# Sample-state updates of a hybrid decoder step: from the shared K/V projection into the third feed-forward

## The chip, the cores and the metric

The kernel runs on one core of a Trainium2 chip. The metric is the device time of one execution in microseconds; the time before is the median of three runs. A TensorE matmul engine (PE), VectorE (DVE), ScalarE (ACT), GpSimd (POOL) and SyncE (SP) run side by side, each with an instruction queue of its own that it takes in order. SP only issues DMAs here; POOL computes and issues DMAs.

## The reference

One inference step of a two-layer decoder over 512 prompt tokens and 8 sample sequences of 4 tokens each, with model width 1024. Each layer is feed-forward, mixer, feed-forward. The mixer of layer 0 is a gated linear attention (GLA) with a recurrent state, that of layer 1 an attention over shared keys and values, which are projected once from the residual stream after layer 0. What matters here is the new GLA state of the samples, an output of the step:

```python
b = jnp.cumsum(gi, axis=2)
b_last = b[:, :, -1:, :]
...
S = jnp.exp(b_last)[:, :, 0, :, None] * S + jnp.einsum('bhcd,bhce->bhde', ki * jnp.exp(b_last - b), vi)
```

For each of 8 sequences and 4 heads a state of 128 x 256 (f32) is scaled by row and a product of keys and values over the 4 tokens is added. The states come from `state_gla` and go to output 6, 4.2 MB each way. Nothing later in the step reads them. The feed-forwards compute `(silu(a) * b) @ w_down` with `a, b = split(u @ w_up)`, and hidden width 2816 = 22 x 128.

## The kernel before, in words

All activations stand with features on the partitions and the 544 tokens (512 + 32) along the free axis, in two halves of 272. Full-precision products are made of three fp32r matmuls, from a high and a low part of each operand: `halves` (L156 to L158) rounds on ACT and subtracts on DVE.

The order of the work is feed-forward "00", GLA, feed-forward "02", shared K/V projection, feed-forward "10", attention, feed-forward "12".

**State work.** `state_stacks` (L1374 to L1386) splits the keys `kts` and the values `vs` of the samples, which GLA left behind, into high and low parts and stacks them on 96 partitions, with 12 casts on DVE (L1384, `kstk`) and 12 on ACT (L1385, `vstk`). `state_step` (L1395) has 16 calls, each with two sequences of one head. At the first call of a head POOL makes the keys masked by sequence, for all 8 sequences at once (L1400, `km`, 96 x 1024, one buffer). For each of two sequences then PE multiplies masked keys with values (L1408, into the PSUM bank `pus`, two banks) and DVE scales the old state and adds (L1409). Every second call stores four states (L1411) and loads the next four but one (L1393), both from POOL's queue; the state tiles hold four sequences, in two buffers.

**Where it stands.** `proj_tokens` (L911) works through five column chunks of the K/V weights with five token blocks each, and runs one of the 16 state steps ahead of each block from the second on (`extra`). What follows a block are the head norms (`norm_heads`, L1437 on: squares on ACT, sums, reciprocal square roots and scaling on DVE, a factor on POOL, and transposes on PE four blocks later) and the stores of keys and values. The weights are loaded by SP and split by `halves` (`hkv`, `lkv`).

**The feed-forward.** `ffn_seven` (L513) treats three of the 22 hidden blocks plainly (the head: `plain_up`, both halves, 6 x 48 matmuls) and the others by a seven-product scheme in place of eight products (`seven`, L679). In the head it also makes sums and differences of the input quarters (`inputs`, L551, and `last_input`, L570). `late` keeps the third of these in short-lived tiles and computes it again in `last_input`, instead of holding it in `t3`. In the main part a hidden block has seven products of 12 matmuls, into five PSUM banks, and after each product `between` (L795) runs some of the down blocks of the round before (each followed by a DVE update of the residual, L398) and a `tick`. `slots` is the number of buffers for the gated values; the sixteen down blocks are spread over the first `7 * (slots - 3)` calls of `between`, 21 at most.

**Steps in a feed-forward.** `steps` are pieces of other work which `tick` (L520) runs: one at each of the first four ticks, and then so many that they are spread evenly over all 139 ticks. The first six ticks are in the head, one after each half of a plain block. Feed-forwards "00" and "02" carry the conditioning projections in this way, with `slots=5, late=True`; "10" has no steps, six slots and is not late.

The instructions are put on each engine's queue by a scheduler that goes by readiness and by program order, so neighbouring parts interleave. A tile of a pool starts when the tile that had its place is done.

Of the kernel before, what the change touches and what calls it, by code (L numbers as in the profile page):

```python
# [9 lines left out]
F32 = mybir.dt.float32  # L10
F32R = mybir.dt.float32r
# [4 lines left out]
ALU = mybir.AluOpType  # L16
AX = mybir.AxisListType

P = 128
# [18 lines left out]
C_SEQ = 640  # L38
# [56 lines left out]
def mod(l, sub, which):  # L95
    return 88 * l + 24 * sub + 8 * which
# [3 lines left out]
def trunk_kernel(ctx: ExitStack, tc: tile.TileContext, a, out, dbg=None, stop=None):  # L100
    nc = tc.nc
    V, S, G, PE, SP = nc.vector, nc.scalar, nc.gpsimd, nc.tensor, nc.sync
# [10 lines left out]
    def aux_bank(name):  # L113
        return pp.tile([P, 512], F32, tag="aux", name=name, bufs=2)
# [21 lines left out]
    cst = keep.tile([P, C_N], F32, name="cst")  # L136
# [50 lines left out]
    ebl = gs_pool.tile([P, 4, 12], F32, name="ebl")  # L187
# [104 lines left out]
    start = ExitStack()  # L292
# [66 lines left out]
    def stats(name, half):  # L359
        t0, t1 = HALF[half]  # L360
        ps = aux_bank(f"st{name}")
        for i, o in enumerate((0, 128, 144)):
            for j in range(3):
                PE.matmul(ps[:, i:i + 1], lhsT=accs[half][j][:, o:o + 128], rhs=ones[:, 0:1], start=j == 0, stop=j == 2)
        x = mean_eps(f"nx{name}", ps[:, 0:3], 3)
        y = rsqrt(x[:], 3, "nr")
        spread(name, y, [(0, P, 0, t0, 128), (1, P, 0, t0 + 128, 128), (2, P, 112, t0 + 256, 16)])
# [39 lines left out]
    def after(name, shift, scale):  # L407
        def f(half):
            stats(f"{name}{half}", half)
            if half:  # L410
                make_u(name, half, shift, scale)
                return []
            return [lambda k=k: make_u(name, half, shift, scale, k, k + 1) for k in range(NB)]
        return f
# [584 lines left out]
    slots = [ada_tile] * 4 + [lo32, hi32] * 2 + [raw_tile] * 2 + [lo32, hi32] * 2 + [ada_tile] * 2  # L999
# [22 lines left out]
    late = [ada_half_loads(v, 1, slots) for v in range(2)]  # L1022
# [349 lines left out]
    stk = {}  # L1372

    def state_stacks(gs_pool2):  # L1374
        kh, kl = (tmp.tile([P, HA], F32R, tag="nv", name=f"kts{i}", bufs=3)[:, 0:P] for i in range(2))
        vh, vl = (tmp.tile([P, HA], F32R, tag="sq", name=f"vs{i}", bufs=3)[:, 0:256] for i in range(2))
        halves(kh, kl, kts[:])
        halves(vh, vl, vs[:])
        ks = gs_pool2.tile([96, 4, P], F32R, name="kstk")
        vt = gs_pool2.tile([96, 4, 256], F32R, name="vstk")  # L1380
        for i, (x, y) in enumerate(((kh, vh), (kh, vl), (kl, vh))):
            for hd in range(4):
                r, o = slice(32 * hd, 32 * hd + 32), slice(32 * i, 32 * i + 32)
                V.tensor_copy(out=ks[o, hd], in_=x[r, :].bitcast(F32))  # L1384
                S.copy(vt[o, hd], y[r, :].bitcast(F32))  # L1385
        stk["k"], stk["v"] = ks, vt  # L1386

    def state_load(gs_pool2, i):
        if i < 8:
            hd, bh = divmod(i, 2)  # L1390
            t = gs_pool2.tile([P, 1024], F32, tag="s1", name=f"s1_{hd}_{bh}", bufs=2)
            stk["s", i] = t[:].rearrange("p (b e) -> p b e", b=4)
            G.dma_start(out=stk["s", i], in_=a["state_gla"][0, 4 * bh:4 * bh + 4, hd].rearrange("b d e -> d b e"))  # L1393

    def state_step(gs_pool2, hd, bh, pr):  # L1395
        if bh == 0 and pr == 0:
            if hd == 0:
                state_stacks(gs_pool2)
            km = gs_pool2.tile([96, 8, P], F32R, tag="km", name=f"km{hd}", bufs=1)
            G.tensor_tensor(out=km[:], in0=stk["k"][:, hd].bitcast(F32).unsqueeze(1).to_broadcast([96, 8, P]),  # L1400
                            in1=cst[0:96, C_SEQ:C_SEQ + 8].unsqueeze(2).to_broadcast([96, 8, P]), op=ALU.mult)
            stk["m"] = km
        st = stk["s", 2 * hd + bh]
        pu = aux_bank(f"pus{hd}_{bh}_{pr}")
        for i in range(2):
            b = 4 * bh + 2 * pr + i
            o = pu[:, i * 256:i * 256 + 256]
            PE.matmul(o, lhsT=stk["m"][:, b], rhs=stk["v"][:, hd], start=True, stop=True)  # L1408
            V.scalar_tensor_tensor(out=st[:, 2 * pr + i], in0=st[:, 2 * pr + i], scalar=ebl[:, hd, 4 + b:5 + b], in1=o, op0=ALU.mult, op1=ALU.add)  # L1409
        if pr:  # L1410
            G.dma_start(out=out[6][0, 4 * bh:4 * bh + 4, hd].rearrange("b d e -> d b e"), in_=st)  # L1411
            state_load(gs_pool2, 2 * hd + bh + 2)

    seq1 = ada_seq(range(11, 20))
    ffn_seven("02", 0, 1, mod(0, 2, 2), after("kv", 72, 80), seq1[:-2], held=seq1[-2:], slots=5, late=True)
# [44 lines left out]
    with ExitStack() as es:  # L1460
        kp = es.enter_context(tc.tile_pool(name="kvt", bufs=1))
        gk = kp.tile([P, 64], F32, name="gk")
        bfv = kp.tile([P, 16], F32, name="bfv")
        SP.dma_start(out=gk[:], in_=a["g_k"].partition_broadcast(P))
        SP.dma_start(out=bfv[:], in_=a["b_f"].partition_broadcast(P))
        ks_out = out[7].rearrange("b t h d -> (b t) (h d)")
        vs_out = out[8].rearrange("b t h d -> (b t) (h d)")
        k_out = out[3][0].rearrange("t h d -> t (h d)")
        v_out = out[4][0].rearrange("t h d -> t (h d)")
        V.memset(lf[:], 0.0)  # L1470

        def evac_kv(ci, t, ps):
            if ci < 2:
                def emit(x, xT):
                    SP.dma_start(out=k_out[t * P:(t + 1) * P, ci * 512:(ci + 1) * 512], in_=x)
                    kx = [kp.tile([P, 512], F32R, tag=f"kx{i}", name=f"kx{ci}_{t}_{i}", bufs=3) for i in range(2)]
                    halves(kx[0][:], kx[1][:], xT)
                    hv, lv = (v[:].bitcast(F32).rearrange("p (k t) -> p k t", k=4) for v in kx)
                    SP.dma_start(out=khscr[:].rearrange("(k p) t -> p k t", p=P)[:, 4 * ci:4 * ci + 4, t * P:(t + 1) * P], in_=hv)
                    for e in range(2):  # L1480
                        SP.dma_start(out=klscr[e::2, 0:64].rearrange("k p t -> p k t")[:, 4 * ci:4 * ci + 4, t * P:(t + 1) * P], in_=lv[64 * e:64 * e + 64])
                return norm_heads(kp, f"k{ci}_{t}", ps, 8, gk, emit)
            c0, w = VC[ci - 2]
            x = kp.tile([P, 352], F32, tag="vx", name=f"vx{ci}_{t}", bufs=2)
            S.copy(x[:, 0:w], ps[:, 0:w])
            SP.dma_start(out=v_out[t * P:(t + 1) * P, c0:c0 + w], in_=x[:, 0:w])
            SP.dma_start(out=vscr[t * P:(t + 1) * P, c0:c0 + w], in_=x[:, 0:w])
            if ci == 4:
                V.tensor_tensor(out=lf[:, t], in0=ps[:, w:w + 16], in1=bfv[:], op=ALU.add)

        def evac_kvs(ci, ps):
            if ci < 2:
                def emit(x, xT):
                    for j in range(4):
                        SP.dma_start(out=ks_out[:, ci * 512 + j * P:ci * 512 + (j + 1) * P], in_=x[32 * j:32 * j + 32])
                    V.tensor_copy(out=kTs[:, 4 * ci:4 * ci + 4], in_=xT.rearrange("p (j t) -> p j t", j=4))
                return norm_heads(kp, f"ks{ci}", ps, 2, gk, emit)
            quads(vnew, ps, *VC[ci - 2])
            if ci == 4:
                V.tensor_tensor(out=lf[0:32, 4], in0=ps[0:32, 256:272], in1=bfv[0:32], op=ALU.add)  # L1500

        gs_pool2 = es.enter_context(tc.tile_pool(name="gsv2", bufs=1))
        for i in range(2):
            state_load(gs_pool2, i)
        st_steps = [lambda hd=hd, bh=bh, pr=pr: state_step(gs_pool2, hd, bh, pr) for hd in range(4) for bh in range(2) for pr in range(2)]
        nv = {(hf, k): kp.tile([P, HA], F32, name=f"nv10_{hf}_{k}") for hf in range(1) for k in range(NB)}
        left = proj_tokens("kv", a["w_kvf"], [[(0, 512)], [(512, 512)], [(1024, 352)], [(1376, 352)], [(1728, 320), (2048, 16)]], evac_kv, evac_kvs, (4, 0, 1, 2, 3), st_steps)
        assert not left
        for (hf, k), v in nv.items():
            scaled(v, hf, mod(1, 0, 1), k)  # L1510
        for hf in range(2):
            make_u("10", hf, mod(1, 0, 0), mod(1, 0, 1), ready=None if hf else nv)
        for j in range(4):
            G.dma_start(out=vs_out[:, 256 * j:256 * j + 256], in_=vnew[32 * j:32 * j + 32, :])
# [62 lines left out]
    if stop == "kv":  # L1577
        return

    ffn_seven("10", 1, 0, mod(1, 0, 2), after("11", mod(1, 1, 0), mod(1, 1, 1)))  # L1580
    dump("h3", h[:])


# [313 lines left out]
```

## Time and profile before

| | |
|---|---|
| median of three runs | 2404.79 us (2399.41 to 2405.72) |
| profiled execution: device time | 2402.91 us |
| its span from first to last instruction | 2401.1 us, mean granted PE clock 0.98 |
| busy: PE, weight loads, DVE, ACT, POOL | 2298.5, 2141.6, 1828.6, 982.0, 923.0 us |
| first and last state matmul (L1408) | start at 1208.5 and 1284.1 us |
| matmuls of the K/V projection | from 1173.1 to 1313.0 us |
| matmuls of feed-forward "10" | from 1313.4 to 1691.5 us |
| DMA bytes in the whole span | 319.45 MB |

A row of a group reads: line, engine, operation, output tile <- input tiles, shape, count | busy us in all, mean ns of one | us in which the engine stood idle just before, and who released it. A row of waits reads: who waited <- for whom: us in all, how many times, the longest. Matmuls are pipelined, so the time from one start to the next is what a matmul costs, and not its duration.

### The profile page before, as it was taken

Reading aid. Unit: us, or ns where it says so; the run is one execution under the profiler, and the core shown is the slowest. Engines: PE = TensorE matmul, PEld = TensorE weight load, DVE = VectorE, ACT = ScalarE, POOL = GpSimd, SP = SyncE. Lnnn points to the kernel's source line nnn. Section 1 sums busy time; section 2 is a strip of 40 time slices with the busy share of each in tenths; the row PEclk is TensorE's granted clock in tenths of the full one; section 3 lists DMA queues with packets and bytes.
Section 4 is the critical chain, followed back from the end, with each engine's and each line's share of the span. In section 5 each row is a group of like instructions: output and inputs, shape, how many; then the busy total and the mean of one; then the engine's idle time right before and its main releaser. Section 6 shows DMA issues by size and latency. Waiting matters only on the chain. (4 is left out here: it accounts for less than half of the span.)

```text
span 2401.1 us, 49301 instructions
## 1 busy us (share of the span) xinstructions
PE 2298.5 (96%) x19292; PEld 2141.6 (89%) x19292; DVE 1828.6 (76%) x3881; ACT 982.0 (41%) x1831; POOL 923.0 (38%) x960
## 2 busy tenths in 40 slices
PE   7999999998999999999989999999999799999999
PEld 6899999987979999999769999999796479999999
DVE  6887777749556987777795988888757667888887
ACT  3343333444533443333524444434436544444432
POOL 0355544207102365444241355543324212455452
PEclk8999999999999999999999999999899899999999
DMA  8535555322172445555467233332146751233322
GB/s 306 172 124 193 192 187 178 114 69 62 54 219 64 141 129 181 187 174 174 144 203 246 81 104 94 99 94 88 47 111 185 157 164 52 78 104 89 102 84 78
DMA packets 356894, 319.45 MB, mean 133 GB/s; under 512 B 25247, under 2 KB 317949, under 8 KB 356614
## 3 DMA queue, kind: packets, MB, share of 16 engines
q1 hardware_dynamic: 341734, 300.24, 40.0%
q0 software_dynamic: 14928, 16.06, 3.0%
q8 instruction: 152, 2.49, 0.4%
q14 instruction: 80, 0.66, 0.1%
HBM read 298.17 MB, written 18.38 MB: 132 GB/s over the span
## 5 line engine op out<-in xcount | busy, mean ns | idle before, releaser
L178 PE MATMUL pd<-gh,ld 128*128 128x272 f32 x1408 | 408.6, 290 | 3.3 <-DVE ld L158 3.3
L176 PE MATMUL pd<-gh,hd 128*128 128x272 f32 x1408 | 409.2, 291 | 2.5 <-ACT hd L157 2.5
L177 PE MATMUL pd<-gl,hd 128*128 128x272 f32 x1408 | 409.3, 291 | 2.2 <-POOL gl L677 2.2
L176 PE MATMUL p<-uh,hu 128*128 128x272 f32 x1216 | 351.8, 289 | 0.0
L177 PE MATMUL p<-ul,hu 128*128 128x272 f32 x1216 | 350.9, 289 | 0.0
L178 PE MATMUL p<-uh,lu 128*128 128x272 f32 x1216 | 350.8, 288 | 0.0
L158 DVE TENSOR_TENSOR lu<-rua,hu 128x512 fp32r<-128x512 f32 (+1 forms) x228 | 272.2, 1194 | 45.9 <-ACT hu L157 37.7
L157 ACT CAST hu<-rua 128x512 fp32r<-128x512 f32 (+1 forms) x228 | 174.0, 763 | 290.4 <-PE p L177 131.8
L398 DVE SCALAR_TENSOR_TENSOR h<-pd,mods,h 128x240 f32<-128x240 f32 (+1 forms) x512 | 240.5, 476 | 49.7 <-PE pd L178 48.9
L178 PEld LDWEIGHTS pd<-gh,ld 128*128 128x128 f32 x1408 | 268.3, 191 | 3.9 <-DVE ld L158 3.9
L176 PEld LDWEIGHTS pd<-gh,hd 128*128 128x128 f32 x1408 | 268.4, 191 | 3.5 <-ACT hd L157 2.7
L177 PEld LDWEIGHTS pd<-gl,hd 128*128 128x128 f32 x1408 | 268.5, 191 | 3.0 <-POOL gl L677 3.0
L176 PE MATMUL p<-th,hu 128*128 128x272 f32 x912 | 264.5, 290 | 1.8 <-ACT th L157 1.8
L178 PE MATMUL p<-th,lu 128*128 128x272 f32 x912 | 264.2, 290 | 0.0
L177 PE MATMUL p<-tl,hu 128*128 128x272 f32 x912 | 264.0, 290 | 0.2 <-DVE tl L158 0.2
L403 POOL TENSOR_TENSOR h<-h,gs 128x32 f32<-128x32 f32 x256 | 127.9, 499 | 333.9 <-DVE gs L401 333.6
L176 PEld LDWEIGHTS p<-uh,hu 128*128 128x128 f32 x1216 | 229.3, 189 | 6.2 <-issue 2.1
L177 PEld LDWEIGHTS p<-ul,hu 128*128 128x128 f32 x1216 | 229.4, 189 | 0.0
L178 PEld LDWEIGHTS p<-uh,lu 128*128 128x128 f32 x1216 | 228.9, 188 | 0.0
L639 POOL TENSOR_TENSOR s<-rua,rub 128x512 f32<-128x512 f32 x76 | 115.1, 1514 | 244.6 <-DMA rub<-in_w_ffn_up_dram 131.3
L645 POOL TENSOR_TENSOR rua<-rub,rua 128x512 f32<-128x512 f32 x76 | 101.2, 1332 | 225.0 <-DVE lu L158 130.2
L176 PEld LDWEIGHTS p<-th,hu 128*128 128x128 f32 x912 | 172.4, 189 | 6.1 <-ACT th L157 2.0
(543 smaller groups left out, 6007.4 us busy)
## 6 DMA issues: line engine op xcount, KB each, us to landing
adaw<-in_w_ada_dram SPq DMA_DIRECT2D x128, 512.0 KB, 4.5
rua<-in_w_ffn_up_dram SPq DMA_DIRECT2D x88, 512.0 KB, 3.9
rub<-in_w_ffn_up_dram SPq DMA_DIRECT2D x88, 512.0 KB, 3.8
rd<-in_w_ffn_down_dram SPq DMA_DIRECT2D x96, 384.0 KB, 3.3
adah<-in_w_ada_dram SPq DMA_DIRECT2D x16, 512.0 KB, 6.3
adaw<-in_w_ada_kv_dram SPq DMA_DIRECT2D x16, 512.0 KB, 8.2
rd<-in_w_ffn_down_dram SPq DMA_DIRECT2D x32, 256.0 KB, 2.7
kp<-in_cache_k_dram SPq DMA_DIRECT2D x16, 512.0 KB, 11.9
```

The source lines that it names most:

```text
L157: S.copy(hi, src)
L158: V.tensor_tensor(out=lo, in0=src, in1=hi.bitcast(F32), op=ALU.subtract)
L176: PE.matmul(ps, lhsT=wh, rhs=xh, start=first and i == 0, stop=False)
L177: PE.matmul(ps, lhsT=wh, rhs=xl, start=False, stop=False)
L178: PE.matmul(ps, lhsT=wl, rhs=xh, start=False, stop=last and i == n - 1)
L398: V.scalar_tensor_tensor(out=h[:, m, t0:p1], in0=ps[:, 0:n], scalar=mods[:, gate + m, 0:1], in1=h[:, m, t0:p1], op0=ALU.mult, op1=ALU.add)
L403: G.tensor_tensor(out=h[:, m, TP:T], in0=h[:, m, TP:T], in1=st[:], op=ALU.add)
L639: G.tensor_tensor(out=o["s3"][:], in0=a11, in1=a21, op=ALU.subtract)
L645: G.tensor_tensor(out=a11, in0=a21, in1=a11, op=ALU.subtract)
```

## The change

The state work leaves the K/V projection and becomes 17 steps of feed-forward "10": the stacks, the first mask and the first two loads, and then sixteen updates of two sequences each. A state tile now holds two sequences, in three buffers; a load is made two updates ahead, from SP's queue instead of POOL's. The mask is made for two sequences (96 x 256), one update ahead, in two buffers. Each update stores its two states, from POOL's queue. Feed-forward "10" gets `slots=5` and `late=True`, and the pool for the state tiles is opened around it.

```diff
     def state_load(gs_pool2, i):
-        if i < 8:
-            hd, bh = divmod(i, 2)
-            t = gs_pool2.tile([P, 1024], F32, tag="s1", name=f"s1_{hd}_{bh}", bufs=2)
-            stk["s", i] = t[:].rearrange("p (b e) -> p b e", b=4)
-            G.dma_start(out=stk["s", i], in_=a["state_gla"][0, 4 * bh:4 * bh + 4, hd].rearrange("b d e -> d b e"))
-
-    def state_step(gs_pool2, hd, bh, pr):
-        if bh == 0 and pr == 0:
-            if hd == 0:
-                state_stacks(gs_pool2)
-            km = gs_pool2.tile([96, 8, P], F32R, tag="km", name=f"km{hd}", bufs=1)
-            G.tensor_tensor(out=km[:], in0=stk["k"][:, hd].bitcast(F32).unsqueeze(1).to_broadcast([96, 8, P]),
-                            in1=cst[0:96, C_SEQ:C_SEQ + 8].unsqueeze(2).to_broadcast([96, 8, P]), op=ALU.mult)
-            stk["m"] = km
-        st = stk["s", 2 * hd + bh]
-        pu = aux_bank(f"pus{hd}_{bh}_{pr}")
+        if i < 16:
+            hd, bp = divmod(i, 4)
+            t = gs_pool2.tile([P, 512], F32, tag="s1", name=f"s1_{i}", bufs=3)
+            stk["s", i] = t[:].rearrange("p (b e) -> p b e", b=2)
+            SP.dma_start(out=stk["s", i], in_=a["state_gla"][0, 2 * bp:2 * bp + 2, hd].rearrange("b d e -> d b e"))
+
+    def state_mask(gs_pool2, i):
+        if i < 16:
+            hd, bp = divmod(i, 4)
+            km = gs_pool2.tile([96, 2, P], F32R, tag="km", name=f"km{i}", bufs=2)
+            G.tensor_tensor(out=km[:], in0=stk["k"][:, hd].bitcast(F32).unsqueeze(1).to_broadcast([96, 2, P]),
+                            in1=cst[0:96, C_SEQ + 2 * bp:C_SEQ + 2 * bp + 2].unsqueeze(2).to_broadcast([96, 2, P]), op=ALU.mult)
+            stk["m", i] = km
+
+    def state_step(gs_pool2, i):
+        hd, bp = divmod(i, 4)
+        st, km = stk["s", i], stk["m", i]
+        pu = aux_bank(f"pus{i}")
+        for j in range(2):
+            o = pu[:, j * 256:j * 256 + 256]
+            PE.matmul(o, lhsT=km[:, j], rhs=stk["v"][:, hd], start=True, stop=True)
+            b = 2 * bp + j
+            V.scalar_tensor_tensor(out=st[:, j], in0=st[:, j], scalar=ebl[:, hd, 4 + b:5 + b], in1=o, op0=ALU.mult, op1=ALU.add)
+        G.dma_start(out=out[6][0, 2 * bp:2 * bp + 2, hd].rearrange("b d e -> d b e"), in_=st)
+        state_mask(gs_pool2, i + 1)
+        state_load(gs_pool2, i + 2)
+
+    def state_start(gs_pool2):
+        state_stacks(gs_pool2)
+        state_mask(gs_pool2, 0)
         for i in range(2):
-            b = 4 * bh + 2 * pr + i
...
-        if pr:
-            G.dma_start(out=out[6][0, 4 * bh:4 * bh + 4, hd].rearrange("b d e -> d b e"), in_=st)
-            state_load(gs_pool2, 2 * hd + bh + 2)
+            state_load(gs_pool2, i)
...
-        gs_pool2 = es.enter_context(tc.tile_pool(name="gsv2", bufs=1))
-        for i in range(2):
-            state_load(gs_pool2, i)
-        st_steps = [lambda hd=hd, bh=bh, pr=pr: state_step(gs_pool2, hd, bh, pr) for hd in range(4) for bh in range(2) for pr in range(2)]
...
-        left = proj_tokens("kv", ..., evac_kv, evac_kvs, (4, 0, 1, 2, 3), st_steps)
+        left = proj_tokens("kv", ..., evac_kv, evac_kvs, (4, 0, 1, 2, 3))
...
-    ffn_seven("10", 1, 0, mod(1, 0, 2), after("11", mod(1, 1, 0), mod(1, 1, 1)))
+    with tc.tile_pool(name="gsv2", bufs=1) as gs_pool2:
+        ffn_seven("10", 1, 0, mod(1, 0, 2), after("11", mod(1, 1, 0), mod(1, 1, 1)),
+                  [lambda: state_start(gs_pool2)] + [lambda i=i: state_step(gs_pool2, i) for i in range(16)], slots=5, late=True)
```

More of the change, by code (lines that the diff above doesn't have):

```diff
@@ L1388, in state_load @@
     def state_load(gs_pool2, i):
-        if i < 8:
-            hd, bh = divmod(i, 2)
-            t = gs_pool2.tile([P, 1024], F32, tag="s1", name=f"s1_{hd}_{bh}", bufs=2)
-            stk["s", i] = t[:].rearrange("p (b e) -> p b e", b=4)
-            G.dma_start(out=stk["s", i], in_=a["state_gla"][0, 4 * bh:4 * bh + 4, hd].rearrange("b d e -> d b e"))
-    def state_step(gs_pool2, hd, bh, pr):
-        if bh == 0 and pr == 0:
-            if hd == 0:
-                state_stacks(gs_pool2)
-            km = gs_pool2.tile([96, 8, P], F32R, tag="km", name=f"km{hd}", bufs=1)
-            G.tensor_tensor(out=km[:], in0=stk["k"][:, hd].bitcast(F32).unsqueeze(1).to_broadcast([96, 8, P]),
-                            in1=cst[0:96, C_SEQ:C_SEQ + 8].unsqueeze(2).to_broadcast([96, 8, P]), op=ALU.mult)
-            stk["m"] = km
-        st = stk["s", 2 * hd + bh]
-        pu = aux_bank(f"pus{hd}_{bh}_{pr}")
-        for i in range(2):
-            b = 4 * bh + 2 * pr + i
-            o = pu[:, i * 256:i * 256 + 256]
-            PE.matmul(o, lhsT=stk["m"][:, b], rhs=stk["v"][:, hd], start=True, stop=True)
-            V.scalar_tensor_tensor(out=st[:, 2 * pr + i], in0=st[:, 2 * pr + i], scalar=ebl[:, hd, 4 + b:5 + b], in1=o, op0=ALU.mult, op1=ALU.add)
-        if pr:
-            G.dma_start(out=out[6][0, 4 * bh:4 * bh + 4, hd].rearrange("b d e -> d b e"), in_=st)
-            state_load(gs_pool2, 2 * hd + bh + 2)
@@ L1500, in evac_kvs @@
                 V.tensor_tensor(out=lf[0:32, 4], in0=ps[0:32, 256:272], in1=bfv[0:32], op=ALU.add)
-        gs_pool2 = es.enter_context(tc.tile_pool(name="gsv2", bufs=1))
-        for i in range(2):
-            state_load(gs_pool2, i)
-        st_steps = [lambda hd=hd, bh=bh, pr=pr: state_step(gs_pool2, hd, bh, pr) for hd in range(4) for bh in range(2) for pr in range(2)]
         nv = {(hf, k): kp.tile([P, HA], F32, name=f"nv10_{hf}_{k}") for hf in range(1) for k in range(NB)}
-        left = proj_tokens("kv", a["w_kvf"], [[(0, 512)], [(512, 512)], [(1024, 352)], [(1376, 352)], [(1728, 320), (2048, 16)]], evac_kv, evac_kvs, (4, 0, 1, 2, 3), st_steps)
+        left = proj_tokens("kv", a["w_kvf"], [[(0, 512)], [(512, 512)], [(1024, 352)], [(1376, 352)], [(1728, 320), (2048, 16)]], evac_kv, evac_kvs, (4, 0, 1, 2, 3))
         assert not left
```

## Prediction, made before the changed kernel was built

> **What bounds the kernel now.** I read the page first, then busy time by stretches, then who waited for whom on TensorE, then the groups of instructions by line. TensorE (PE) is busy 96% of the span on the page, so a change can gain only where PE waits or runs at a low clock. The stretches below cover the shared K/V projection (from 1200), the plain head of the third feed-forward (1313 to 1353), the rest of it (1353 to 1692), and, for comparison, the head and the rest of the second feed-forward (754 to 1171).
>
> ```profile
> span 2401.1 us, 49301 instructions
> ...
> 1200.00:1250.00 50.00, 42.29 (x245) 32.72 (x244) 48.28 (x158) 13.81 (x22) 20.25 (x18) 0.97 0.64 200
> 1250.00:1284.00 34.00, 27.76 (x209) 25.75 (x208) 18.99 (x53) 6.94 (x12) 9.35 (x10) 0.90 0.80 258
> 1284.00:1313.00 29.00, 29.00 (x308) 28.32 (x308) 13.76 (x34) 12.37 (x25) 3.61 (x6) 1.00 0.80 247
> 1313.00:1353.00 40.00, 40.00 (x318) 39.80 (x316) 38.70 (x77) 19.09 (x40) 10.98 (x6) 1.00 0.32 93
> 1353.00:1692.00 339.00, 336.09 (x2645) 335.42 (x2644) 282.81 (x501) 138.97 (x236) 163.72 (x173) 0.99 0.31 92
> 754.00:801.00 47.00, 44.92 (x375) 40.70 (x374) 44.15 (x102) 19.80 (x45) 10.81 (x9) 1.00 0.45 152
> 801.00:1171.00 370.00, 368.67 (x3139) 352.29 (x3139) 287.95 (x529) 141.94 (x245) 174.74 (x172) 1.00 0.50 164
> ```
>
> The columns are stretch, length, then busy time of PE, weight loads, DVE, ACT and POOL, then the granted clock, the DMA share and GB/s. In the projection PE is idle 50.0 - 42.3 = 7.7 us and 34.0 - 27.8 = 6.2 us, 13.9 in all, up to 1284, where the state steps end. After that, with the same projection still running, it is idle 0.0 of 29 us. The third feed-forward is bound by PE almost throughout. In its head PE and DVE are both full (40.0 and 38.7 of 40), which is the weak spot of the place that the work is moved to. The next two views are PE's waits in the projection and the groups of the state work.
>
> ```profile
> PE pus L1408 <- DVE s L1409: 8.6, 7, 2.8
> PE pus L1408 <- POOL km L1400: 3.2, 2, 2.6
> PE pus L1408 <- DVE hssk L1447: 2.0, 1, 2.0
> ```
> ```profile
> L1408 PE MATMUL pus<-vstk,km 96*128 96x256 f32 x32 | 11.2, 357 | 14.0 <-DVE s L1409 8.6 <-POOL km L1400 3.2 <-DVE hssk L1447 2.0
> ...
> L1409 DVE SCALAR_TENSOR_TENSOR s<-s,ebl,pus 128x256 f32<-128x256 f32 x32 | 15.2, 476 | 9.7 <-PE pus L1408 7.3 <-DMA s<-in_state_gla_dram 2.4
> L1384 DVE CAST kstk<-kts 32x128 fp32r<-32x128 f32 x12 | 5.2, 436 | 0.2
> L1400 POOL TENSOR_TENSOR km<-kstk,cst 96x1024 fp32r<-96x1024 f32 x4 | 7.8, 1955 | 5.2 <-PE pus L1408 4.1 <-DVE kstk L1384 1.1
> ```
>
> Every wait of PE in the projection after 1200 us stands before a state matmul (pus): 14.0 us over ten waits. PE takes its queue in order, so projection matmuls that were ready stood behind them. The "DVE s" waits are for the bank that the step before has still to read out; that DVE instruction was itself late behind the head norms (DVE 48.3 of 50) or behind a state load.
>
> **What leaves the projection.** First the waits, 14.0 us. Second, PE runs slowly for a while after the two longest of them. This timeline of PE shows start, length and line.
>
> ```profile
> 1204.60 0.39 PE L975 MATMUL kv<-lkv,uh 128*128 128x512 f32 x1
> 1204.83 0.39 PE L976 MATMUL kv<-hkv,ul 128*128 128x512 f32 x1
> ...
> 1208.47 0.80 PE L1408 MATMUL pus<-vstk,km 96*128 96x256 f32 x2 [2.56 <-POOL km L1400]
> 1209.07 0.63 PE L974 MATMUL kv<-hkv,uh 128*128 128x512 f32 x1
> ...
> 1210.78 0.63 PE L975 MATMUL kv<-lkv,uh 128*128 128x512 f32 x1
> ...
> 1226.96 0.28 PE L1408 MATMUL pus<-vstk,km 96*128 96x256 f32 x1
> 1227.08 0.40 PE L975 MATMUL kv<-lkv,uh 128*128 128x512 f32 x1
> ```
> ```profile
> 1277.34 0.58 PE L1408 MATMUL pus<-vstk,km 96*128 96x256 f32 x1 [2.83 <-DVE s L1409]
> 1277.72 0.50 PE L976 MATMUL kv<-hkv,ul 128*128 128x352 f32 x1
> ...
> 1283.00 0.39 PE L976 MATMUL kv<-hkv,ul 128*128 128x352 f32 x1
> ...
> 1283.52 0.32 PE L975 MATMUL kv<-lkv,uh 128*128 128x352 f32 x1
> 1283.68 0.32 PE L976 MATMUL kv<-hkv,ul 128*128 128x352 f32 x1
> ```
>
> A 128x512 matmul follows the last by 0.23 us at 1204, but four steps from 1209.07 to 1210.78 take 0.43 each: 5 x 0.20 = 1.0 us lost. After the wait of 2.83 us, 18 steps from 1277.72 to 1283.00 take 0.293 each against 0.16 at 1283.5: 18 x 0.13 = 2.4 us lost. So 3.4 us beside the waits; the granted clock of 0.90 in that stretch fits. The Trainium skill ("TensorE: Matmul & The Clock Gate", Part 1) says that the clock falls back after an idle window of about 3.4 us. This case's trace shows the slow pace after waits of 2.56 and 2.83 us, so the measurement is shorter; by the page these two waits would not have cost the clock, the 3.4 us would go for another reason or stay, and the time would be 2394 instead of 2391.
>
> Third, PE loses the 32 state matmuls themselves. One is followed after 1227.08 - 1226.96 = 0.12 us, so 32 x 0.12 = 3.8 us go here and come back in the feed-forward: zero in sum. The matmul count of the projection is otherwise unchanged.
>
> What is late next in the projection? DVE loses 15.2 + 5.2 us of its 67 in 1200 to 1284, which leaves some 47 us of DVE work for a PE stretch of 84 - 14 - 3.4 - 3.8 = 63 us. The stretch from 1284 on shows that PE stays full without the steps, while weights are still arriving at a DMA share of 0.80. I take the whole 17.4 us; the lower bound is 13, if a quarter of the waits turns into waits for norms or weights.
>
> **What arrives in the feed-forward, after its head.** The rule for ticks gives one step at each of the first four ticks (the stacks, then steps 0 to 2), all in the plain head; the remaining 13 steps come one every 8 of 139 ticks, that is every 20 us (339 us hold 19 x 7 = 133 ticks). There PE gets 26 x 0.12 = 3.1 us (counted above), DVE 26 x 0.476 = 12.4 us where it has 339 - 283 = 56 us idle, POOL one mask of 1955/4 = 0.49 us and one store issue a step where it is busy 164 of 339. A mask made one step ahead and a state loaded two steps ahead have 20 and 40 us. So a step finds its mask, state and bank, and I cost it at nothing more. If that cover fails, each step costs a wait (second rival).
>
> ```profile
> s<-in_state_gla_dram POOLq DMA_DIRECT2D x8, 512.0 KB, 5.5
> out_dram<-s POOLq DMA_DIRECT2D x8, 512.0 KB, 4.5
> ```
>
> The loads move to SP's queue, among the weight loads. Load 3 reuses the buffer of step 0 and so waits for step 0's store, which lands in 4.5 us or less (half the size); in the head, where steps follow each other within a plain block, SP can stand for up to that long with the weights of block 2 behind it. This is part of the head's range. Later the store is 20 us old.
>
> The feed-forward also becomes "late" with five buffers of gated values instead of six. The second feed-forward already runs so, with 18 conditioning steps in it.
>
> ```profile
> PE adat L243 <- ACT adar L240: 1.4, 2, 0.8
> PE st L364 <- ACT sq L351: 0.7, 1, 0.7
> PE pd L177 <- POOL gl L677: 0.4, 1, 0.4
> PE pa L177 <- DVE ul L392: 0.4, 2, 0.2
> PE pa L176 <- ACT uh L391: 0.4, 1, 0.4
> ```
>
> Over 754 to 1171 PE waited 3.3 us in all, and for the down blocks, which the smaller buffer bunches into the first two thirds of a round, 0.4. I put nothing down for the buffers.
>
> **The head, where the cost is.** DVE gets there the twelve casts (5.2 us with the delays that they met, 2.6 at their least), two small subtractions (under 1 us), six updates (6 x 0.476 = 2.9), and the late form of the inputs.
>
> ```profile
> L546 DVE TENSOR_TENSOR x<-uh,ul 128x272 f32<-128x272 f32 x12 | 5.0, 436 | 0.0
> ...
> L539 DVE TENSOR_TENSOR t<-x,t 128x272 f32<-128x272 f32 x4 | 1.7, 435 | 0.0
> L539 DVE TENSOR_TENSOR ul<-t,uh 128x1088 fp32r<-128x1088 f32 x1 | 1.3, 1292 | 0.3 <-ACT uh L572 0.3
> ```
> ```profile
> PE pd L178 <- DVE ld L158: 0.5, 1, 0.5
> ```
>
> Late means 16 more instructions of this size (4 blocks x two sums, a difference and a low part), 16 x 0.436 = 7.0, and without the four of 1.7 and the long one of 1.3: 4.0 us more. Together 5.2 + 0.7 + 2.9 + 4.0 = 12.8 us on a DVE that is full, where PE already waits 0.5 us for it (ld). Not all of it reaches PE: five product banks are free to fill, and a bank's 12 matmuls take 12 x 0.127 = 1.5 us (339 us over 2,645 records), 7.5 us in all; and the last late inputs are needed only by the fourth product. That leaves 12.8 - 7.5 = 5.3; I take 5 us, with 0 and 13 as the ends. The zero end is the second feed-forward's head, which carries the late inputs at 44.2 of 47 us of DVE with PE waits of 2 us; there conditioning matmuls gave PE something to do meanwhile, so I don't take it. A gain below zero is excluded, since PE has no wait in this head to lose but 0.5 us.
>
> The Trainium skill ("SBUF — State Buffer", Who interferes with whom) says that a DVE instruction with two SBUF inputs and a GpSimd one that reads SBUF exclude each other. The head's four masks would then hold DVE up by 4 x 0.49 = 2.0 us more, and the time by it would be 2393; no row here isolates that.
>
> **The sum.** -14.0 - 3.4 + 5.0 = -12.4 us on the profiled execution's 2402.91 gives 2390.5. The median of the three runs, 2404.79, is 1.9 above that execution, which gives 2392.4. I say 2391, a gain of 0.57%.
>
> **The rivals.** *The head eats the gain.* DVE falls behind by all of the 12.8 us and PE waits for all of it: -17.4 + 12.8 = -4.6, 2398 to 2400, within 0.3%, which is about what a measurement of this kernel can tell from no change. For it: DVE at 38.7 of 40, and the chain that ended last runs over DVE in the head. Against it: the second feed-forward's head. 0.24.
>
> *The waits move with the steps (slower).* A state matmul still stands in PE's queue in order, and POOL now makes sixteen masks and issues sixteen stores, each store waiting for DVE with the next mask and the low parts of the gated values behind it on POOL. In the projection ten waits cost 17.4 us with their slow clock, 1.74 each. If each of sixteen steps waits once at that price, 27.8 us come back, with the head's 5 the result is +15.4: 2418 to 2420. It is slower by 0.3% from (17.4 - 5.0 + 7.2)/16 = 1.2 us a step on. Against it: the lead of 20 us, and the second feed-forward, where 18 steps with their own loads cost 1.4 us at the transposes. 0.08.
>
> *The steps don't spread.* Engine queues are ordered by a scheduler; if it pulls the steps together the prefetch is lost and the sum falls between the two rivals, about zero to +7. 0.02.
>
> **How the numbers follow.** The forecast case, a gain over 7.2 us, has 0.66. It spans 2383 (head at zero: 2402.9 - 17.4 = 2385.5, and 2 to 3 us for the scatter of 2399.41 to 2405.72) to 2397. The first rival takes the range to 2401. Chances: faster 0.66, within 0.3% 0.25 (the first rival and a part of the third), slower 0.09.
>
> **What would show it.** Right: no PE wait over 1 us in the projection after its start and a granted clock near 1.00, its stretch some 21 us shorter (with the matmuls); PE waits of about 5 us in the feed-forward's head with DVE as the releaser; single pus matmuls of 0.12 us every 20 us after it. Wrong: pus rows with idle before them in the feed-forward, projection waits that now name lkv or hssk, weight loads in the head that land late behind a state load, or a head longer by over 8 us.

## The result, and the profile after

The changed kernel takes 2412.89 us (median of 20 runs, 2408.35 to 2420.97), beside 2403.98 us for the kernel before (20 runs, 2393.99 to 2411.14). The ratio is 1.0038 [1.0029, 1.0048]: slower by about 9 us, where 2391 was forecast. The profiled execution after took 2410.93 us, with a span of 2409.1. The balance below is made between the two profiled spans, 2401.1 and 2409.1.

The first view is busy time by stretches of the kernel after, with the columns of the prediction: twice the K/V projection (up to 1293), then the plain head of feed-forward "10" (1293 to 1342) and the rest of it (up to 1704).

```profile
span 2409.1 us, 49332 instructions
...
1200.00:1250.00 50.00, 49.67 (x360) 41.72 (x359) 45.36 (x172) 16.31 (x27) 11.79 (x11) 1.00 0.54 169
1250.00:1293.00 43.00, 41.17 (x379) 39.43 (x378) 19.31 (x42) 18.50 (x34) 2.83 (x5) 1.00 0.83 249
1293.00:1342.00 49.00, 41.69 (x301) 41.25 (x300) 45.91 (x98) 24.03 (x54) 14.78 (x14) 0.90 0.40 123
1342.00:1704.00 362.00, 347.05 (x2693) 343.95 (x2692) 293.99 (x537) 138.14 (x235) 188.48 (x194) 0.98 0.34 103
```

The projection is what was forecast: PE is idle 0.3 of 50 us and 1.8 of 43, at a full clock. The head of the feed-forward is the new bad place. PE is idle 49.00 - 41.69 = 7.3 us there and the granted clock is 0.90, where PE stood full at 1.00 before. The rest has 15 us of idle time, where it had 2.9 in 339.

The waits of PE in feed-forward "10" (1293 to 1704) of the kernel after, in us in all, times and longest, name the largest item:

```profile
PE pus L1409 <- DVE s L1411: 15.5, 8, 4.1
PE st L364 <- POOL sq L355: 2.8, 1, 2.8
PE pd L176 <- ACT gh L676: 2.6, 2, 2.3
PE pd L177 <- POOL gl L677: 1.3, 3, 0.5
```

The wait of a state matmul for DVE's update (`s`), which was 8.6 us in seven waits in the projection before (of 14.0 us before state matmuls in all), is 15.5 us in eight waits in the feed-forward.

| stretch by its first and last matmul, us | before | after | after, less before |
|---|---|---|---|
| start to the end of feed-forward "02" (same code) | 1171.0 | 1174.0 | +3.0 |
| K/V projection | 142.4 | 119.3 | -23.1 |
| head of "10" | 36.2 | 48.4 | +12.2 |
| rest of "10" | 341.8 | 362.5 | +20.7 |
| attention | 319.4 | 313.2 | -6.2 |
| feed-forward "12" | 390.3 | 391.7 | +1.4 |
| span | 2401.1 | 2409.1 | +8.0 |

These are single executions: the 3.0 us in the first row, where both kernels run the same code, show how far two of them can differ without any change.

What the projection gives (23.1, of which 3.8 are the moved matmuls) feed-forward "10" takes back with interest (32.9). Its 32.9 us are: 15.5 of waits before state matmuls; 32 x 0.12 = 3.8 of the matmuls themselves; 3.9 - 0.6 = 3.3 more of waits for the gated values (`gh`, `gl`), which before were one wait of 0.6; 2.8 - 1.5 = 1.3 at a sum of squares (`st`); and 7.7 of slow clock. The last was summed over the timeline: for each 128x272 matmul with no wait of its own that follows another such matmul by 0.16 to 0.32 us, the time above the usual 0.125. That makes about 9.7 us after and 2.0 before. Together 31.6 of 32.9. The attention's part is taken up at the end.

**Why PE waits.** The timeline of PE (start, length, line) after, in the head:

```profile
1305.37 0.28 PE L1409 MATMUL pus<-vstk,km 96*128 96x256 f32 x1
...
1306.48 0.29 PE L178 MATMUL pa<-uh,lua 128*128 128x272 f32 x1
1310.87 0.58 PE L1409 MATMUL pus<-vstk,km 96*128 96x256 f32 x1 [4.10 <-DVE s L1411]
1311.25 0.43 PE L176 MATMUL pa<-uh,hua 128*128 128x272 f32 x1
1311.48 0.43 PE L177 MATMUL pa<-ul,hua 128*128 128x272 f32 x1
```

And DVE in the same microseconds:

```profile
1303.80 1.22 DVE L158 TENSOR_TENSOR lua<-rua,hua 128x1024 fp32r<-128x1024 f32 x1
1304.94 0.43 DVE L539 TENSOR_TENSOR x<-x,x 128x272 f32<-128x272 f32 x1
1305.29 2.31 DVE L158 TENSOR_TENSOR lub<-rub,hub 128x1024 fp32r<-128x1024 f32 x1
1307.53 1.50 DVE L158 TENSOR_TENSOR tl<-x,th 128x272 fp32r<-128x272 f32 x1
...
1310.35 0.47 DVE L1411 SCALAR_TENSOR_TENSOR s<-s,ebl,pus 128x256 f32<-128x256 f32 x1
```

The two matmuls of one step go into the two halves of one PSUM bank, and between them, in program order, stands DVE's update that reads the first half. The second matmul waits for that update. It isn't the step before that holds the bank, as the prediction has it, but the first half of the same step: the matmul at 1305.37 runs without a wait, its update starts at 1310.35 behind nearly five microseconds of DVE's own queue, and the second matmul at 1310.87, nine feed-forward matmuls later, finds it just done. All eight waits are of this kind: each ends some 0.5 us after the start of the update of the same step's first half. No lead of mask or state helps against that, since both were there. The Trainium skill ("PSUM — Partial Sum Buffer", PSUM bank collisions raise a hardware error) says that the compiler back end's scheduler puts a dependency between any two instructions on different engines that touch one bank and partition quarter, and that a different address in the bank does not help; the order seen here fits that, with up to 4.1 us a time.

The rows of the kernel before would have shown it. Its timelines of PE and of DVE have, ahead of the row at 1277.34 which the prediction quotes:

```profile
1273.34 0.36 PE L1408 MATMUL pus<-vstk,km 96*128 96x256 f32 x1
```
```profile
1276.80 0.48 DVE L1409 SCALAR_TENSOR_TENSOR s<-s,ebl,pus 128x256 f32<-128x256 f32 x1 [1.47 <-DMA s<-in_state_gla_dram]
```

The matmul at 1273.34 is the first of the pair and the one at 1277.34 the second; the update between them was late by its state load. Matched in this way by their starts, six of the seven waits for `s` before (8.2 of 8.6 us) are inside a pair. Only the one of 0.40 us, at 1240.91, is for the step before.

### The profile page after: what moved, and what is told of

Its sections match the earlier page's. It is cut to its first block, busy times and chain, and to the rows that moved or that the text cites. A ratio compares the mean times of both kernels' runs of the same rounds, so it can differ in the third digit from the quotient of the medians.

```text
span 2409.1 us, 49332 instructions
## 1 busy us (share of the span) xinstructions
PE 2304.1 (96%) x19292; PEld 2148.4 (89%) x19292; DVE 1828.5 (76%) x3892; ACT 983.0 (41%) x1834; POOL 931.3 (39%) x972
## 4 chain that ended last, share of the span: by engine, by line
PE 72%; DVE 13%; issue 4%; DMA 4%; POOL 4%; ACT 3%; SPq 1%; DVEq 0%; POOLq 0%; ACTq 0%
PE p L176 9%; PE p L177 9%; PE p L178 9%; PE pd L177 6%; PE pd L178 6%; PE pd L176 6%; PE ada L236 2%; DVE lu L158 2%; DMA kd<-khscr 1%; DVE nv L372 1%; POOL rua L645 1%; ACT hu L157 1%; PE st L364 1%; DVE x L546 1%; DVE ul L392 1%
## 5 line engine op out<-in xcount | busy, mean ns | idle before, releaser
L158 DVE TENSOR_TENSOR lu<-rua,hu 128x512 fp32r<-128x512 f32 (+1 forms) x228 | 271.4, 1190 | 46.6 <-ACT hu L157 36.6
```

The source lines that it names most:

```text
L158: V.tensor_tensor(out=lo, in0=src, in1=hi.bitcast(F32), op=ALU.subtract)
```

## The experiments

Ratios are to the kernel before, run on the same chip. There is no experiment 4. Experiments 1, 2, 3 and 5 shared one chip (before: median 2404.71), 6 to 9 a second (2403.81), 10 to 13 a third (2404.0). Theory A: the order inside the pair makes the waits. Rivals: the head's DVE load and the late inputs; five buffers in place of six; the loads on SP's queue.

**1. The pair's order in the kernel after.** Both matmuls first, then both updates.

```diff
         for j in range(2):
-            o = pu[:, j * 256:j * 256 + 256]
-            PE.matmul(o, lhsT=km[:, j], rhs=stk["v"][:, hd], start=True, stop=True)
+            PE.matmul(pu[:, j * 256:j * 256 + 256], lhsT=km[:, j], rhs=stk["v"][:, hd], start=True, stop=True)
+        for j in range(2):
             b = 2 * bp + j
-            V.scalar_tensor_tensor(out=st[:, j], ..., in1=o, op0=ALU.mult, op1=ALU.add)
+            V.scalar_tensor_tensor(out=st[:, j], ..., in1=pu[:, j * 256:j * 256 + 256], op0=ALU.mult, op1=ALU.add)
```

> The changed kernel, with the two state matmuls of a step issued first and the two updates on VectorE after them. Theory A (the bank): the second matmul of a pair waits for VectorE to read the first one's result, because both lie in one PSUM bank and each update is issued between the matmuls; TensorE, in order, stands behind VectorE's queue. Then the 15.5 us of waits before pus in the feed-forward and the slow matmuls after them go, some 15 to 24 us: 2389 to 2398 us, and no pus row has idle time named after the update L1411 or its successor. Rival B (VectorE is too full): the waits are VectorE's backlog and come back under other names (tl, ul, ld, gh): 2405 to 2413 us, the head of the feed-forward still about 48 us long.

Measured: 1.0003 [0.9988, 1.0017], 2406.15 us. The timeline of PE shows the same step of the head as one pair of 0.24 us (1306.76 - 1306.52), without a wait:

```profile
1306.52 0.40 PE L1408 MATMUL pus<-vstk,km 96*128 96x256 f32 x2
1306.76 0.29 PE L176 MATMUL pa<-uh,hua 128*128 128x272 f32 x1
```

The head falls from 48.4 to 36.9 us: exactly the 36.2 of before and six state matmuls (0.7). DVE carries the same casts, updates and late inputs there, with 36.66 of 36.9 us busy. So DVE's load in the head cost PE time there only by way of the pair wait. The head does what theory A says, but the time lies in the range of rival B: the total gained only (1.0038 - 1.0003) x 2404 = 8 us on the kernel after, since the rest of the feed-forward got longer, from 362.5 to 366.4 in the profiled executions. PE's waits in feed-forward "10" of this kernel:

```profile
PE pd L176 <- ACT hd L157: 6.2, 1, 6.2
PE pd L176 <- ACT gh L676: 4.1, 4, 1.6
PE st L364 <- POOL sq L355: 2.6, 1, 2.6
PE pd L177 <- POOL gl L677: 2.3, 5, 0.5
```

All waits before state matmuls are gone, and other work is late next: the first down weights (`hd`), and the gated values at the starts of the rounds (`gh`, `gl`). With the moved matmuls and a slow clock of 7.9 us (2.0 before) these make most of what the rest of "10" is longer than before. Experiments 3 and 6 to 10 look for their cause.

**2. The same order in the kernel before.** Same edit in its `state_step`.

> The kernel before, with the same order of a pair (two matmuls, then two updates), the state steps still in the K/V projection. Theory A: of the 14.0 us of waits there the 8.6 us named after the update go, and the slow clock after the longest (2.4 us); those for the mask and the norms (5.2 us) stay: 2393 to 2395 us against 2404. Rival B: VectorE is full in the projection and each wait moves to the next pair or to the norms: 2401 to 2404 us.

Measured: 0.9967 [0.9950, 0.9985], 2399.64 us, between the ranges of theory A and rival B. The gain doesn't lie where theory A would have it. The projection went from 142.4 to 140.9 us only. The attention, where nothing was changed, went from 319.4 to 314.8, which is more than the 3.5 us between the two spans (2401.1 and 2397.6). PE's waits in its projection:

```profile
PE pus L1406 <- POOL km L1400: 4.0, 2, 2.8
PE pus L1406 <- DVE s L1409: 3.7, 4, 2.2
...
PE pus L1406 <- DVE kx L158: 2.5, 1, 2.5
PE pus L1406 <- DVE h2w L151: 2.0, 1, 2.0
```

The waits for `s` fell from 8.6 to 3.7 us, and the matmuls then waited for the mask and for the norms instead (`kx`, `h2w`). The four waits for `s` that are left (3.7 us) end with the update of an earlier step, as at 1228.27, where the matmuls of one step start right after the update at 1227.74 that ends the step before: with the pair in order, the wait that the prediction had in mind comes to light. So in the projection other things were nearly as late, and one cure only made room for the next wait. What the pair's order is worth in time there, this run doesn't show.

**3 and 8. The kernel before with the new form of the feed-forward, without steps.** First five buffers and late inputs together, then five buffers alone.

```diff
-    ffn_seven("10", 1, 0, mod(1, 0, 2), after("11", mod(1, 1, 0), mod(1, 1, 1)))
+    ffn_seven("10", 1, 0, mod(1, 0, 2), after("11", mod(1, 1, 0), mod(1, 1, 1)), slots=5, late=True)
```

> The kernel before with the state steps in the K/V projection, and only the third feed-forward made late with five buffers. Theory A: these two cost nearly nothing, as in the second feed-forward: 2403 to 2407 us, head up to 39 us. Rival B: the late inputs overfill VectorE in the head and make the larger part of the 12.2 us by which the head grew: 2410 to 2416 us, head over 44 us.

> The kernel before with only the five buffers in the third feed-forward, not late, states in the projection. With five buffers the first down block of a round follows one product after the last hidden block, and stood 0.45 us for gl at five rounds in e3, with slow matmuls after it. Theory slots: most of the 7 us by which the main part grew in e3 is this: 2408 to 2411 us against 2404.7, gl waits of about 2.2 us in all. Theory late: the late inputs made it, through hd: 2403 to 2406 us.

Measured: 1.0035 [1.0017, 1.0054], 2411.61 us, with both; 1.0035 [1.0018, 1.0053], 2413.96 us, with `slots=5` alone. The late inputs cost nothing that these intervals (about 0.2% either way) can show, the five buffers 0.35%, some 8 us. The head is 36.2 us in both, as before, so rival B of experiment 3 (a head over 44 us) falls; the time of experiment 3 lies in its range, but by the buffers, as experiment 8 shows. In the profiled execution with five buffers alone the rest is 345.9 us instead of 341.8. Among its waits in feed-forward "10":

```profile
PE pd L177 <- POOL gl L677: 2.3, 5, 0.5
PE pd L176 <- ACT hd L157: 2.0, 1, 2.0
```

The code says why. With six buffers the sixteen down blocks spread over 21 calls of `between`, and after the first product 16 x 1 // 21 = 0 blocks are due. With five they spread over 14, and 16 x 1 // 14 = 1 is due: the round's first down block follows one product after the hidden block that makes its last input, so `gl` or `hd` isn't there. The profile shows 4.1 us of loss in the one execution that was traced, which at 2406.31 us is one of the shorter ones; the ratio over all says 8, and what makes up the difference wasn't traced.

**5. The changed kernel without its steps.**

> The changed kernel without any state work: the samples' new states (output 6) are not computed or stored, while the projection without steps and the late feed-forward with five buffers stay as in the change. Its distance to the changed kernel is all that the steps cost in the feed-forward. Theory A: 2413 less 33 us (12.2 of the head and 20.6 of the rest) is 2380, at most 3 more for the late head: 2380 to 2384 us. Rival B: a late head that costs 8 us or more by itself: 2388 to 2394 us.

```diff
-                  [lambda: state_start(gs_pool2)] + [lambda i=i: state_step(gs_pool2, i) for i in range(16)], slots=5, late=True)
+                  [], slots=5, late=True)
```

This kernel leaves out the samples' new states (output 6). Measured: 0.9906 [0.9880, 0.9931], 2379.93 us. So the state work in the feed-forward costs 2412.89 - 2379.93 = 33 us in the kernel after, of which the matmuls are 3.8.

**6. The loads back on POOL's queue**, with the order of experiment 1 (`G.dma_start` in place of `SP.dma_start` in `state_load`). It asks whether the wait of 6.2 us for `hd` comes from state loads ahead of the weight loads on SP's queue.

> The kernel of e1_pair_order with the state loads issued from POOL's queue again instead of SP's. In e1 TensorE stood 6.2 us at the first down block for weights (hd) that had landed late. Theory SP: loads 2 to 4, which wait on SP for a store, held up the weight loads behind them; then the wait goes, with the slow matmuls after it: 6 to 9 us below e1, 2397 to 2400 us. Theory DVE: the weight load itself waited for a raw buffer that VectorE's backlog (stacks, updates, late inputs) freed late; then the wait stays, over 4 us, and the time too: 2404 to 2408 us.

Measured: 1.0080 [1.0057, 1.0103], 2421.34 us, far above both expected ranges. PE's waits in feed-forward "10":

```profile
PE pd L176 <- ACT gh L676: 7.0, 3, 3.8
PE pd L177 <- POOL gl L677: 6.6, 5, 5.0
PE pd L176 <- ACT hd L157: 5.2, 1, 5.2
```

`hd` is still 5.2 us late, so SP's queue is not its main cause. The waits for the gated values grew from 6.4 to 13.6 us; they come from POOL's queue (`gl`) and from ACT (`gh`), and the likely reason, which was not tested, is that POOL now stands before loads until a state tile is free (17.2 us of waiting for stores from 1290 to 1710). The queue that the change chose was the better one. SP's own waits in experiment 1, around the head, show what can hold `hd` up:

```profile
SPq L1393 <- DMA out_dram<-s: 22.9, 3, 8.7
...
SPq L721 <- DVE lu L158: 4.9, 2, 3.3
```

SP does stand 22.9 us for stores of the states, as the prediction feared for load 3, but the down weights' load (L721) waits in addition for a raw buffer that DVE frees with the low parts (`lu`), and DVE has a backlog. The timelines tell the two apart: in experiment 6, with no state load on SP, the first of these weight loads is still issued only at 1331.23, right after the low part that DVE starts at 1329.88 and that takes 1.21 us; in experiment 1 it is issued at 1335.24, after one that starts at 1333.88.

**7. No steps in the head**, with the order of experiment 1: `tick` runs only what the even spread asks for (`min(total, ticks[0], early)` with `early=0`).

> The kernel of e1_pair_order with no step forced at the first four ticks: the 17 steps are spread evenly from tick 9 on, so that the head holds no state work. Theory DVE: VectorE's backlog in the head shrinks by the stacks and six updates (some 7 us) and the 6.2 us wait for hd falls to the 0.8 to 2.0 us that the late head alone had: 2397 to 2401 us. Theory SP gives the same wait gone, as no load waits for a young store; together with e6 it tells them apart. If instead the wait only moves to the stacks in the main part, 2404 to 2408.

Measured: 1.0034 [1.0020, 1.0049], 2411.11 us: a clear miss of the expected 2397 to 2401. `hd` did fall from 6.2 to 1.8 us, with its weight load issued at 1321.80; together with experiment 6 this puts its lateness down to DVE's backlog in the head. The head was 36.2 us. But the stacks now run in the first round of down blocks (casts from 1337.8 to 1346.2), which takes 58.5 us, only 1.6 less than in experiment 1, and the gated values are later at the starts of the rounds behind it:

```profile
PE pd L176 <- ACT gh L676: 6.1, 5, 1.8
PE pd L177 <- POOL gl L677: 2.7, 5, 0.9
```

**9 and 10. The down blocks one product later.** Experiment 9 is 7 with this, 10 the kernel before with `slots=5` and this.

```diff
-                    while gone[0] < min(2 * NB * done[0] // n, 2 * NB):
+                    while gone[0] < min(2 * NB * (done[0] - lag) // (n - lag), 2 * NB):
```

> The kernel of e7_no_early_steps with the down blocks of a round starting one product later (spread over products 2 to 14 of the round instead of 1 to 14). If gh and gl waits at the round starts (6.4 us in e1) and the slow matmuls after them are the rest of the loss, they go: 2388 to 2393 us, main part 348 to 352 us. If they are an expression of a VectorE that is too full with state updates, they move to the second block or to the products: within 3 us of e7.

> The kernel of e8_before_slots5 (before, five buffers) with the down blocks of a round starting one product later. If the cost of five buffers is the first down block that stands right behind the last hidden block of its round, the gl waits (2.3 us in e8) go, the main part falls from 345.9 to 342 to 343 us and the ratio to before is 0.999 to 1.001. If the cost is the bunching of the sixteen blocks, it stays at 1.003.

Measured: experiment 9 0.9973 [0.9958, 0.9989], 2397.5 us, which is 14 us below experiment 7, though not the 2388 to 2393 expected; experiment 10 0.9994 [0.9978, 1.0009], 2402.43 us, as expected. The whole cost of the five buffers is gone with `lag=1`. PE's waits in feed-forward "10" of experiment 10 are these two, with no `gl`, `gh` or `hd`:

```profile
PE st L364 <- POOL sq L355: 1.5, 1, 1.5
PE pd L178 <- DVE ld L158: 0.4, 1, 0.4
```

**11, 12 and 13. The parts together.** 11 is the kernel after with `lag=1` alone; 13 has the pair's order and `lag=1`, and four early steps as in the change; 12 is 13 with one early step (the stacks).

> The changed kernel with only that later start, the pairs in their old order (matmul, update, matmul, update). The gh and gl waits (3.9 us) and the slow matmuls after them go; the waits before the second matmul of a pair (15.5 us) stay: 2405 to 2409 us. Under 2402 the round starts were the larger loss and the pairs the smaller; at 2411 or more the later start does nothing.

> The kernel of e9_lag with the stacks back at the first tick, in the head, and the sixteen steps spread over the main part. In e9 the stacks fell into the first round and TensorE waited some 8 us around it (1340 to 1398); in the head the casts had cost it nothing in e1. Expected 2389 to 2394 us, ratio 0.993 to 0.997, main part 350 to 355 us. If VectorE's backlog simply moves with the casts, 2396 to 2400.

> The kernel of e1_pair_order with the later start of the down blocks, and the four early steps left as in the change. The first down block comes later by a product, which also shortens the 6.2 us wait for hd. Expected 2394 to 2399 us, ratio 0.995 to 0.998; if the early updates are what costs there, it is 4 us or more above e12.

| | pair as in the change | both matmuls first |
|---|---|---|
| down blocks as in the change | 1.0038 [1.0029, 1.0048] | 1.0003 [0.9988, 1.0017] (1) |
| one product later | 1.0011 [0.9998, 1.0025] (11) | 0.9950 [0.9937, 0.9963] (13) |

Experiment 12 gave 0.9965 [0.9953, 0.9977], 2395.99 us, and 13 took 2392.88 us, faster than both kernels; 11 took 2405.59 us, as expected, 12 was 2 us above its range and 13 some 1 us below. Alone, the order is worth 0.35% and the lag 0.27%; together 0.88%, more than their sum by 0.26%, which is about what these intervals allow. A reason for more than the sum is in the rows of experiment 1: with the pair cured, time is lost at `gh`, `gl` and `hd`, and the lag shortens these. PE's waits in feed-forward "10", first of experiment 11 and then of 13:

```profile
PE pus L1409 <- DVE s L1411: 13.8, 10, 4.1
```
```profile
PE pd L176 <- ACT hd L157: 3.0, 2, 2.7
PE st L364 <- POOL sq L355: 2.6, 1, 2.6
PE pd L177 <- POOL gl L677: 1.3, 3, 0.4
...
PE pd L176 <- ACT gh L676: 0.7, 1, 0.7
```

With the lag alone the pair's waits stay at 13.8 us; with both, `hd` is 3.0 instead of 6.2 and the two gated values 2.0 instead of 6.4. The feed-forward of experiment 13 takes 36.9 + 355.2 us, 14.1 more than before, and the projection 120.5, which is 21.9 less. Of the 14.1 us, 3.8 are the state matmuls and 9.5 - 2.6 = 6.9 longer waits; most of the rest is slow clock. Steps in the head are no harm once the pair is in order: with four early steps the ratio is 0.9950, with none (9, on another chip) 0.9973.

## Why the prediction was wrong, by its steps

- *"First the waits, 14.0 us", the slow clock, and the moved matmuls* (some 21 us from the projection): right. It became 23.1 us shorter, with a granted clock of 1.00, and from 1200 us on PE is idle 0.3 + 1.8 = 2.2 us of 93. Nothing else was late next, as forecast: the lower bound of 13 wasn't reached.
- *"The 'DVE s' waits are for the bank that the step before has still to read out"*: wrong for 8.2 of the 8.6 us, and the error from which the cost of nothing for a step comes. The wait is inside the pair. Its length is DVE's backlog when the step runs, so it goes with the steps wherever they go.
- *"So a step finds its mask, state and bank, and I cost it at nothing more"*: this step of the sum failed. Mask and state were there; the bank wasn't. Eight waits of 15.5 us (7.3 in the head, 8.2 after it) came, and 6.6 us of slow steps stand right behind four of them (4.10, 3.21, 2.06 and 2.29). Experiment 1 is the proof: with the two updates behind the two matmuls all of them are gone.
- *The head, +5 us (0 to 13), as DVE's extra 12.8 us less 7.5 of slack*: it measured +12.2, inside the range by luck, since the mechanism is another: two pair waits (7.3 us) and the slow clock after them (3.5). Experiment 1 has the same DVE work and a head of 36.9 us; what remains is 0.7 of matmuls. DVE's backlog did matter, but at the first down weights behind the head (6.2 us in experiment 1, 1.8 without early steps), a place that the prediction didn't look at.
- *"I put nothing down for the buffers"*: the second failed step. Five buffers alone cost 0.35%. The second feed-forward, from which it concluded, seems to hide the early down block behind its conditioning matmuls, which the prediction itself noticed for the head and didn't apply here. In the timeline before, its round start at 852.64 has no such matmul among or just ahead of the eight products before it and waits the same 0.44 us for `gl`; the four from 905.60 to 1073.18 have one and don't wait. No experiment tested this. The late inputs, for which it put down 4.0 us of DVE, cost nothing that could be measured (3 against 8).
- *The loads on SP's queue*: the mechanism (SP standing for a store) was seen, 24.1 us of it around the head of the kernel after; no wait of PE was traced to it, and the other queue is worse (1.0080).
- *The rivals.* "The waits move with the steps" had 0.08 and was right in kind, though not by the reason that it gives (POOL's masks and stores), since all eight waits name DVE's update: slower from 1.2 us a step, and measured (15.5 + 7.7) / 16 = 1.45, if all the added slow clock is counted to the steps; it is somewhat less, since experiment 1, with no such wait, still shows 7.9 us of slow steps in all. It forecast 2418 to 2420; in the balance of the two profiled executions the attention's 6.2 us are most of the way down to 2413. "The head eats the gain" fell: the head's DVE load alone ate nothing. The steps did spread.
- *The attention*, -6.2 us, wasn't in the sum. It is the wait for `kd`, a load from scratch memory. Among PE's waits there, before and after:

```profile
PE fs L1776 <- DMA kd<-khscr: 13.6, 2, 9.3
```
```profile
PE fs L1782 <- DMA kd<-khscr: 7.7, 2, 4.2
```

It is 11.9 us in experiment 2 and 11.9 in experiment 13, 9.1 in experiment 1. So it isn't simply a gift of the removed state work, and what sets it stays open. At the attention's start the kernel after has a wait of 4.4 us for a POOL instruction (L1546, `rs`) ahead of a sum of squares; all kernels traced here with steps in feed-forward "10" have it, and none without. It costs little in the balance, since the kernel before waits 3.8 us at the same place for `diag` (1.9) and `sq` (1.9). Nothing was tried on it.
- *The sum.* With the two failed steps mended, experiment 13 takes 2392.88 us, beside the forecast of 2391. That it comes so near is in part luck: its projection gives 21.9 us as forecast, but its feed-forward takes 14.1 more than before, where the sum has 8.8 (the 5 us of the head and 3.8 of matmuls).

## What to carry to other kernels

A wait for "the engine that reads the bank" can be for the other half of the same instruction pair: find the two matmuls in the timeline and look at what stands between them in program order before you assume that distance in time will cure it. Two matmuls into one bank go ahead of both reads. And when a stage's parameter is taken over from a place where other work hid its cost, count what hides it in the new place: here it was enough to begin the down blocks one product later.

## What the hardware showed

PE's clock falls after short waits. In the wait of 4.10 us above it falls before the wait is over: the granted clock of the kernel after is 0.50 from 1309.0 to 1310.8, where PE still stands, and 1.00 again from 1316. Behind this wait 19 steps from 1311.25 to 1315.55 take 0.226 us each in place of 0.125, 1.9 us lost; after one of only 2.06 us the timeline of the kernel after has the same pace, for 15 steps:

```profile
1496.22 0.41 PE L1409 MATMUL pus<-vstk,km 96*128 96x256 f32 x1 [2.06 <-DVE s L1411]
1496.44 0.42 PE L176 MATMUL p<-th,hu 128*128 128x272 f32 x1
1496.66 0.43 PE L177 MATMUL p<-tl,hu 128*128 128x272 f32 x1
```

After one of 2.29 us, at 1556.62, the next step takes 0.22 us and those behind it 0.125, until the slow pace comes a microsecond later. So the length of the wait alone doesn't decide it, and a wait of 2 us can cost 3.5. The Trainium skill ("TensorE: Matmul & The Clock Gate", Part 1) gives about 3.4 us for the idle window and says that it runs freely: the trace has the slow pace after less, and an irregular one, which would fit a window that starts where it will. In feed-forward "10" the slow steps cost about 9.7 us in the kernel after and 2.0 before.

DVE slows beside POOL. In the timeline of DVE above, one 128x1024 low part (both inputs in SBUF) takes 1.22 us (`lua`) and the next one 2.31 (`lub`), and a 128x272 one (`tl`) 1.50 where its peers take 0.43. POOL in those microseconds, same kernel:

```profile
1304.97 1.54 POOL L639 TENSOR_TENSOR s<-rua,rub 128x512 f32<-128x512 f32 x1 [2.34 <-DMA rub<-in_w_ffn_up_dram]
1306.60 2.13 POOL L640 TENSOR_TENSOR rub<-rub 128x512 f32<-128x512 f32 x1
```

The two slow instructions stand beside these two sums of weights, and 1.09 + 1.07 = 2.2 of the 4.1 us of the first wait in the head are theirs, if the rest of DVE's queue would have moved up. In all of feed-forward "10" of the kernel after, 128x272 low parts (L158) with no POOL instruction beside them take at most 0.44 us (16 of them), and those that overlap one up to 1.52; the 128x272 additions of L671, which take one input from PSUM, take at most 0.44 with or without POOL (68 and 65 of them). The Trainium skill's rule on the shared port ("SBUF — State Buffer", Who interferes with whom), which the prediction applied to the masks alone, fits: the weight sums pay it. In the head such slow rows lose DVE about 6 us in the kernel before as well as after, so they aren't what the change added, and that the 2.2 us are near the 2.0 that the prediction gave for the masks is chance.
